# An attention round on TensorE: the transposes of the probabilities move behind the projections' step

## The chip, the core and the metric

The kernel runs on one core of one Trainium2 chip. The time is device microseconds of one execution of the whole kernel; lower is better. TensorE is called PE below, its weight loads PEld, VectorE DVE, ScalarE ACT, GpSimd POOL and SyncE SP, as in the profile.

## What is computed

One encoder layer with two parallel branches is applied to a prompt of 1024 tokens and, with the same weights, to a sample of 512 tokens; the model width is 1024. The part that the change touches is branch B, a windowed attention with three dilations (1, 4 and 16), 8 heads of width 64 each. Cut to what matters, for one dilation:

```python
logits = einsum('bghnqe,bghnke->bghnqk', qr, kb) + bias        # windows of 64 + 2*64 keys
mx = max(where(mask, logits, -inf), -1)
p = exp(logits - mx[..., None]); den = sum(p, -1)
o = einsum('bghnqk,bghnke->bghnqe', p, vb)                     # unnormalised; mixed over the dilations later
```

Around it stand one wide input projection `h @ w_in` (about 9700 columns), branch A (a bidirectional mLSTM scan in chunks of 128 tokens), gates, two output projections, a last projection and two RMS norms.

## The kernel before, in words

**Stages.** The prompt ("A", 1024 tokens) is projected first. From about 1000 us on, `body` (L1906 on) runs five stages in turn: mLSTM of A (L1951), attention of A (L1956), mLSTM of the sample "B" (L1967), attention of B (L1980), and the mixing of B's dilations with what is left (L1984 on). The two attention stages lie at about 1316 to 1636 us and 1846 to 2112 us of the span.

**Fill.** These stages have little work for PE between their dependent steps. So `Fill` (L114) holds a list of other units of work, projections of the sample and output projections of both inputs, each cut into steps; `fill(share)` (L171) advances a running target by a share of the stage's rate and issues as many steps as that makes due. One step is a product of three matmuls (`mm3`, L206: high by high, low by high and high by low part of fp32r pairs), of 512, 430 or 426 columns. A is given 260 steps for 96 rounds, B 290 for 48 (`STEPS`, L1751, and L1427). A unit of weights is loaded by DMA into `wraw` (L261), then split: ACT rounds it to `wh` (L272) and DVE subtracts (`wl`, L278). `split_w` (L264) makes the two wait in issue order for the last few attention instructions, which are kept in `held`.

**A tile of attention.** `attention` (L1304) makes tiles of 128 queries of two heads, with 256 keys ("wide": dilations 1 and 4 of A, dilation 1 of B) or 128 keys. Each has four stages:

- stage 0, `products` (L1354): on PE, the logits into the PSUM tile `lg` (L1362, or `mm3` through L209 to L211).
- stage 1, `softmax` (L1369): on DVE bias and maximum for each head (L1374) and the negated maximum `nm` (L1376); on ACT the two exponentials into `ls` (L1378).
- stage 2, `turn` (L1381): on PE 4 transposes (2 for a narrow tile) of `ls` into the PSUM tile `pt` (L1385); then one copy `pts` out of PSUM, on DVE for even tiles (L1390) and on ACT for odd ones (L1388).
- stage 3, `output` (L1393): on PE the products with the values into `o` (L1398), which read `pts`; on ACT the copy `ot` out of PSUM (L1400); then a DMA is queued.

**A round.** `attend` (L1408) appends one tile per round and calls `att_round` (L1473), which gives each of the last four tiles one stage: the newest its stage 0, the one before its stage 1, then 2 and 3; `fill(1)` is one more entry of that list. 12 units of 8 tiles make 96 rounds in A, 12 of 4 make 48 in B, and three more rounds drain the pipeline of each.

**What sets the order.** In these stages PE and SP keep the order in which the program issues (`manual_schedule`, L1907). DVE, ACT and POOL are put in order by a scheduler ahead of the run, by its own estimate of when each instruction can start; at run time every engine works through its list in order. `lg`, `pt` and `o` have two PSUM buffers each, `pts` two and `ls` three in SBUF. In attention A one more generator, `lanes` (L923), is advanced by four of the rounds (L1462): it works out the gates of B's mLSTM with small instructions on PE, ACT and DVE (L934 to L1008).

Of the kernel before, what the change touches and what calls it, by code (L numbers as in the profile page):

```python
# [181 lines left out]
class Net:  # L182
# [1289 lines left out]

    def att_round(self, tiles, fill):  # L1473

        for age, stage in ((0, 0), (1, 1), (2, 2), (None, None), (3, 3)):
            if age is None:
                fill(1)
            elif age < len(tiles) and tiles[-1 - age] is not None:
                tiles[-1 - age][stage]()
# [571 lines left out]
```

## Time and profile before

| what | value |
| --- | --- |
| time, three runs | 2256.5, 2256.57 and 2256.66 us (median 2256.57) |
| span of the profiled execution, first to last instruction | 2259.7 us, 3.1 us over the median of the timed runs |
| PE busy | 2244.2 us, 99% of the span |
| PEld, DVE, ACT, POOL busy | 1964.6, 1509.5, 1129.2, 718.6 us |
| granted PE clock | 1.000 |
| transposes L1385 in both attention stages | 71.9 us of PE (union of their records) |
| value products L1398 in both | 115.4 us of PE |
| PE idle in attention A, in attention B | 0.24 us of 320, 1.19 us of 266 |

The profile is of one execution. A row of its timeline has the start, the duration, the engine, the source line, the operation, the tile written and the tiles read, the shape, how many instructions were merged into the row, and in brackets how long the engine stood idle before it and what ended that. The duration of a matmul reaches to its modelled end, and the next one starts before it; what PE spends on one is read from start to start.

### The profile page before, as it was taken

The page shows a single profiled execution, that of the slowest core. Times are in us where ns is not written, and L with a number is a line of the kernel's source. Part 1 is how long each engine was busy: PE and PEld are TensorE (multiplying, and loading weights), DVE is VectorE, ACT ScalarE, POOL GpSimd, SP SyncE. Part 2 cuts the span into 40 slices and gives each one's busy share as a digit, 9 for nine tenths or more (in the row PEclk, how much of TensorE's full clock was granted, in tenths as well). Part 3 has the DMA queues.
Part 4 walks back from the last instruction along what each step waited for, and adds up shares of the span by engine and source line. Part 5 has one row for each costly group of instructions (what it writes and reads, how often), then busy time and mean ns, then how long its engine had stood idle before and what let it go on. Part 6 is the DMA issues. An engine that isn't in the chain of part 4 may idle for free.

```text
span 2259.7 us, 35388 instructions
## 1 busy us (share of the span) xinstructions
PE 2244.2 (99%) x12226; PEld 1964.6 (87%) x12226; DVE 1509.5 (67%) x2875; ACT 1129.2 (50%) x2369; POOL 718.6 (32%) x1000
## 2 busy tenths in 40 slices
PE   9999999999999999999999999999999999999998
PEld 8999888888888888888888899999888888888887
DVE  7765577687776556558887755544689844655674
ACT  6432244344444434357777655566665644554332
POOL 1000333333333223237676610011165522221221
PEclk9999999999999999999999999999999999999999
DMA  3652455543332223284664789997678797776663
GB/s 123 168 134 76 172 205 192 192 176 121 112 111 103 84 84 140 103 298 153 226 223 127 191 217 235 253 245 221 203 248 284 238 278 211 233 251 200 233 230 109
DMA packets 222685, 418.27 MB, mean 185 GB/s; under 512 B 24841, under 2 KB 128969, under 8 KB 222506
## 3 DMA queue, kind: packets, MB, share of 16 engines
q1 hardware_dynamic: 194536, 315.86, 44.4%
q0 software_dynamic: 24368, 87.56, 12.4%
q10 hardware_dynamic: 3602, 12.59, 1.4%
q8 instruction: 97, 1.59, 0.3%
q14 instruction: 82, 0.67, 0.1%
HBM read 296.19 MB, written 128.12 MB: 188 GB/s over the span
## 4 chain that ended last, share of the span: by engine, by line
PE 95%; DMA 2%; issue 1%; ACT 1%; POOL 1%; DVE 0%; DVEq 0%; SPq 0%; POOLq 0%; ACTq 0%
PE d L211 14%; PE d L209 14%; PE d L210 14%; PE dense L209 12%; PE dense L211 12%; PE dense L210 12%; PE o L1398 4%; PE pt L1385 2%; PE lg L1362 2%; PE num L211 1%; PE num L209 1%; PE num L210 1%; PE kv L209 1%; PE a L1070 1%; PE kv L210 1%
## 5 line engine op out<-in xcount | busy, mean ns | idle before, releaser
L209 PE MATMUL dense<-H,wh 128*128 128x512 f32 x664 | 270.6, 408 | 0.8 <-DVE V0b L1643 0.8
L211 PE MATMUL dense<-H,wl 128*128 128x512 f32 x664 | 260.9, 393 | 0.0
L210 PE MATMUL dense<-H,wh 128*128 128x512 f32 x664 | 260.2, 392 | 0.0
L210 PE MATMUL d<-Hl,phla 128*128 128x512 f32 x608 | 236.5, 389 | 0.0
L211 PE MATMUL d<-Hh,phla 128*128 128x512 f32 x608 | 236.5, 389 | 0.0
L209 PE MATMUL d<-Hh,phla 128*128 128x512 f32 x608 | 236.5, 389 | 0.0
L278 DVE TENSOR_TENSOR wl<-wraw,wh 128x1024 fp32r<-128x1024 f32 (+1 forms) x121 | 149.3, 1234 | 70.0 <-ACT wh L272 69.9
L1374 DVE CUSTOM_DVE_ANT_0 ls<-lg,bias 128x256 f32<-128x256 f32 (+1 forms) x288 | 93.7, 362 | 132.8 <-PE lg L1362 71.2
L211 PE MATMUL d<-Hh,phlb 128*128 128x512 f32 x456 | 177.4, 389 | 0.0
L209 PE MATMUL d<-Hh,phlb 128*128 128x512 f32 x456 | 177.4, 389 | 0.0
L210 PE MATMUL d<-Hl,phlb 128*128 128x512 f32 x456 | 177.4, 389 | 0.0
L687 POOL TENSOR_TENSOR psum_w<-pw_raw 128x512 f32<-128x512 f32 x38 | 58.0, 1527 | 365.1 <-DMA pw_raw<-w_in 208.8
L1378 ACT ACTIVATE ls<-ls,nm 128x256 f32<-128x256 f32 (+1 forms) x288 | 130.3, 454 | 84.0 <-DVE nm L1376 59.2
L272 ACT ACTIVATE wh<-wraw 128x1024 fp32r<-128x1024 f32 (+1 forms) x124 | 128.7, 1038 | 77.1 <-PE dense L210 27.0
L211 PEld LDWEIGHTS dense<-H,wl 128*128 128x128 f32 x664 | 124.6, 188 | 28.2
L209 PE MATMUL d<-vhi,Hh 128*128 128x322 f32 x448 | 140.9, 315 | 0.3
L211 PE MATMUL d<-vhi,Hl 128*128 128x322 f32 x448 | 140.3, 313 | 0.4 <-DVE Hl L396 0.2
L210 PE MATMUL d<-vlo,Hh 128*128 128x322 f32 x448 | 139.7, 312 | 0.0
L209 PEld LDWEIGHTS dense<-H,wh 128*128 128x128 f32 x664 | 125.0, 188 | 15.5 <-DVE V0b L1643 1.2
L210 PEld LDWEIGHTS dense<-H,wh 128*128 128x128 f32 x664 | 125.4, 189 | 14.3
L211 PEld LDWEIGHTS d<-Hh,phla 128*128 128x128 f32 x608 | 114.1, 188 | 23.7
L210 PEld LDWEIGHTS d<-Hl,phla 128*128 128x128 f32 x608 | 114.2, 188 | 23.6
(570 smaller groups left out, 6166.4 us busy)
## 6 DMA issues: line engine op xcount, KB each, us to landing
pw_raw<-w_in SPq DMA_DIRECT2D x76, 512.0 KB
wraw<-w_in SPq DMA_DIRECT2D x64, 512.0 KB
aqk_a<-pwk SPq DMA_DIRECT2D x48, 512.0 KB
aqk_b<-sw SPq DMA_DIRECT2D x48, 256.0 KB
wraw<-w_pm POOLq DMA_DIRECT2D x24, 512.0 KB, 6.1
wraw<-w_out POOLq DMA_DIRECT2D x24, 512.0 KB, 4.0
wraw<-w_v POOLq DMA_DIRECT2D x22, 430.0 KB, 7.3
erep<-erow SPq DMA_DIRECT2D x16, 512.0 KB
```

Of the source, the lines that this page charges most:

```text
L209: nc.tensor.matmul(out, lh, rh, start=start, stop=False)
L210: nc.tensor.matmul(out, lh, rl, start=False, stop=False)
L211: nc.tensor.matmul(out, ll, rh, start=False, stop=stop)
L272: high = nc.scalar.activation(hi[:, :n], raw[:, :n], AF.Copy)
L278: low = (self.lows or nc.vector).tensor_sub(lo[:, :n], raw[:, :n], hi[:, :n].bitcast(F32))
L687: self.nc.gpsimd.tensor_add(s[:, 0], ws[1][:, 0], ws[1][:, 1])
L1070: nc.tensor.matmul(p[:, c - c0], kT[:, ct, c * P:(c + 1) * P], qT[:, ct, c * P:(c + 1) * P], start=ct == 0, stop=ct == 1)
L1362: nc.tensor.matmul(lg[:, hh, c:c + w], q[hh][:, qs], z[:, k0:k0 + w], start=z is k[hh], stop=z is not k[hh])
L1374: nc.vector.tensor_tensor_reduce(out=ls[:, hh], in0=ts["lg"][hh], in1=bt[:, hh], scale=1.0, scalar=NEG, op0=OP.add, op1=OP.max, accum_out= ...
L1378: self.held = self.held[-3:] + [nc.scalar.activation(ls[:, hh], ls[:, hh], AF.Exp, bias=nm[:, hh:hh + 1], accum_out=ot[:, 128 + hh:129 + hh])]
L1385: nc.tensor.transpose(pp[:, hh * nk + x], ts["ls"][:, hh, x * P:(x + 1) * P], self.ident)
L1398: nc.tensor.matmul(po[:, hh * 64:hh * 64 + 64], pt[:, hh * nk + x], v[:, kt[x], c0 + hh * 64:c0 + hh * 64 + 64], start=x == 0, stop=x == n ...
```

## The change

One entry of the list in `att_round` moves. Before, PE's order in a round was logits of the newest tile, transposes of the tile two older, the projections' step (`fill(1)`), value products of the tile three older. After, it is logits, projections' step, transposes, value products. The stages' ages, the buffers, the DMAs and all shapes stay as they are.

```diff
     def att_round(self, tiles, fill):
 
-        for age, stage in ((0, 0), (1, 1), (2, 2), (None, None), (3, 3)):
+        for age, stage in ((0, 0), (1, 1), (None, None), (2, 2), (3, 3)):
             if age is None:
                 fill(1)
             elif age < len(tiles) and tiles[-1 - age] is not None:
                 tiles[-1 - age][stage]()
```

Compared instruction by instruction, the built programs have the same number of PE instructions with the transposes moved, SP's list is the same, and the lists of ACT, DVE and POOL hold the same work in a somewhat different order.

## The prediction

> **What bounds the kernel now.** I read the page's head, its chain of work, the busy time by stage, and PE's own waits.
>
> ```profile
> span 2259.7 us, 35388 instructions
> PE 95%; DMA 2%; issue 1%; ACT 1%; POOL 1%; DVE 0%; DVEq 0%; SPq 0%; POOLq 0%; ACTq 0%
> ```
>
> ```profile
> 1316.00:1636.00 320.00, 319.76 (x2157) 304.63 (x2156) 166.31 (x627) 204.39 (x637) 34.21 (x67) 1.00 0.88 234
> 1846.00:2112.00 266.00, 264.81 (x1426) 226.92 (x1427) 155.69 (x402) 132.55 (x362) 64.98 (x124) 1.00 0.72 223
> ```
>
> ```profile
> PE num L211 <- POOL scl L1110: 1.2, 1, 1.2
> PE dense L209 <- DVE V0b L1643: 0.8, 1, 0.8
> PE o L1398 <- ACT pts L1388: 0.2, 1, 0.2
> ```
>
> PE is 95% of the chain that ends last. The second fence has the two attention stages, its columns busy PE, PEld, DVE, ACT, POOL, then PE's clock and the DMA share: PE idles 0.24 us in A's stage and 1.19 us in B's. The third has what PE's waits say of these stages and the start of the mLSTM behind A's. So PE streams without a hole in nearly all of the 144 rounds (96 in A, 48 in B). A new order can gain only these 1.4 us, unless the matmuls themselves get cheaper side by side; it can lose wherever it opens a hole, one for one, since nothing but PE is on the chain. A reported time should follow the span: the profiled one is 2259.7 us, 3.1 us over the median of 2256.57 us, and I add the sum to the median.
>
> **What the change removes, adds and moves.** No instruction goes or comes. On PE the transposes pass the round's projection steps. Three costs follow: what PE pays at the new seams, what the value products wait for, and what the altered lists of ACT, DVE and POOL delay. SP's list, with every DMA that it issues, is unchanged.
>
> *Seams.* One round of A, PE's rows, the middle of the fill left out:
>
> ```profile
> 1400.12 1.00 PE L1398 MATMUL o<-K,pts 128*128 128x64 f32 x8
> 1400.93 0.36 PE L1362 MATMUL lg<-V1a,Q 128*128 128x256 f32 x1
> 1401.13 0.28 PE L1362 MATMUL lg<-V1b,Q 128*128 128x256 f32 x1
> ...
> 1401.48 0.60 PE L1385 MATMUL pt<-ident,ls 128*128 128x128 f32 x4
> 1401.84 0.44 PE L209 MATMUL dense<-wh,H 128*128 128x430 f32 x1
> 1402.12 0.36 PE L210 MATMUL dense<-wl,H 128*128 128x430 f32 x1
> 1402.32 0.36 PE L211 MATMUL dense<-wh,H 128*128 128x430 f32 x1
> ```
>
> Steady, a 430-column matmul takes 0.20 us from start to start (1402.12 to 1402.32). From the first transpose to the second step matmul lie 0.64 us (1401.48 to 1402.12); less 0.20 for the first step matmul, 0.44 is left: 0.11 for each of four transposes, the last too. From the first value product to the second logits matmul lie 1.01 us; less 0.12 for the first logits matmul (256 columns), 0.89 is left, 0.11 for each of eight. So the group pays its own slots and no more on leaving. The seam that the change makes, transposes straight into f32 products, is found in the opening stage:
>
> ```profile
> 35.58 0.27 PE L428 MATMUL d<-ident,x 128*128 128x128 f32 x1
> 35.69 0.39 PE L430 MATMUL d<-Hl,x 128*128 128x128 f32 x2
> 35.91 0.27 PE L428 MATMUL d<-ident,x 128*128 128x128 f32 x1
> 36.02 0.39 PE L430 MATMUL d<-Hl,x 128*128 128x128 f32 x2
> ```
>
> There a transpose (L428) and an f32 product (L430, two records) take turns, 0.33 us for the three, 0.11 each: no price in either direction. The seams are taken at 0; the bounds are in the rivals.
>
> *What the products wait for.* They need `pts`, copied out of PSUM after the transposes. Before, two fills lie between transposes and products of a tile; after, one.
>
> ```profile
> 1404.47 0.60 PE L1385 MATMUL pt<-ident,ls 128*128 128x128 f32 x4
> 1406.67 1.00 PE L1398 MATMUL o<-K,pts 128*128 128x64 f32 x8
> 1410.23 0.33 PE L1398 MATMUL o<-K,pts 128*128 128x64 f32 x2
> ```
>
> ```profile
> 1405.36 0.69 DVE L1390 COPY pts<-pt 128x512 f32<-128x512 f32 x1
> ```
>
> This tile's transposes start at 1404.47, its copy ends at 1406.05 (1.58 us later, and that behind DVE's softmax of another tile), its products start at 1410.23. After, the transposes stand just ahead of the other tile's products, 0.44 us before 1406.67, at 1406.23: 4.00 us are left for 1.58, so 2.4 us are spare. The narrow rounds of A are shortest:
>
> ```profile
> 1551.71 0.55 PE L1398 MATMUL o<-K,pts 128*128 128x64 f32 x4
> 1552.51 0.38 PE L1385 MATMUL pt<-ident,ls 128*128 128x128 f32 x2
> 1553.89 0.56 PE L1398 MATMUL o<-K,pts 128*128 128x64 f32 x4
> ```
>
> ```profile
> 1553.23 0.42 DVE L1390 COPY pts<-pt 128x256 f32<-128x256 f32 x1
> ```
>
> From transposes to end of copy 1.14 us; a round of 2.18 us plus 0.22 for the two transposes gives 2.40, spare 1.26. B's rounds last 5.5 us on the mean (266 by 48), so more is spare. In an ordinary round the change costs nothing, and what hides the copy is one fill in place of two. In exchange the exponentials get a fill more ahead of the transposes, which no PE wait asks for.
>
> *Where one fill doesn't do.* A late copy already shows once, where the `lanes` work sits on ACT:
>
> ```profile
> 1465.59 0.58 ACT L1388 ACTIVATE pts<-pt 128x512 f32<-128x512 f32 x1
> 1466.56 0.51 ACT L1378 ACTIVATE ls<-ls,nm 128x256 f32<-128x256 f32 x1 [0.39 <-DVE nm L1376]
> ...
> 1467.56 0.26 ACT L1400 ACTIVATE ot<-o 128x128 f32<-128x128 f32 x1
> ...
> 1473.21 1.28 ACT L945 ACT_TABLE_LOAD   x1
> 1474.51 0.31 ACT L945 ACTIVATE l_e<-l_l 64x128 f32<-64x128 f32 x1
> 1474.72 0.58 ACT L1388 ACTIVATE pts<-pt 128x512 f32<-128x512 f32 x1
> 1475.25 0.51 ACT L1378 ACTIVATE ls<-ls,nm 128x256 f32<-128x256 f32 x1
> ...
> 1476.25 0.26 ACT L1400 ACTIVATE ot<-o 128x128 f32<-128x128 f32 x1
> ```
>
> ```profile
> 1475.35 1.10 PE L1398 MATMUL o<-K,pts 128*128 128x64 f32 x8 [0.24 <-ACT pts L1388]
> ```
>
> The products at 1475.35 start as this copy ends (1474.72 and 0.58). In the changed program's list the copy stands behind the two exponentials of the tile two younger, which take 1475.25 to 1476.25: 1.0 us later. The copy of two tiles earlier (1465.59) likewise moves behind its two exponentials, out of a place with 0.39 us of idle time behind it ahead of work that may run without a gap to 1474.72: by an estimate from those rows about 0.5 us more for all behind it. Together PE waits about **1.5 us** longer here. Between 0.9 (the second shift absorbed) and 2.4 us (the tile of the first copy misses its products too, by one more evicting instruction). Behind the late products on PE stand the next logits and steps; who waits for those is late by as much, and PE's stream is simply shifted.
>
> *POOL's list.* It differs in three places; one is near PE, where B's mLSTM begins.
>
> ```profile
> 1639.58 0.59 POOL L250 DMA_DIRECT2D sraw<-ym_a  x1 [9.30 <-ACT st L1072]
> ...
> 1641.94 0.46 POOL L1110 TENSOR_TENSOR scl<-rm,sch 128x128 fp32r<-128x128 f32 x1 [0.57 <-ACT sch L1109]
> ...
> 1643.40 1.44 POOL L1118 TENSOR_TENSOR ql<-qw,qh 128x256 fp32r<-128x256 f32 x2 [0.63 <-ACT qh L1117]
> ```
>
> ```profile
> 1644.26 0.28 PE L211 MATMUL num<-V0a,scl 128*128 128x258 f32 x1
> ```
>
> After, the DMA issue that waits until 1639.58 stands ahead of the first mask and product, and one `ql` ahead of that `scl`. `ql` can't start before about 1643.3 (here it waits for ACT until 1643.40), takes 0.72, then `scl` 0.46: 1644.5 or later, against a need at 1644.26. I take **0.4 us**, between 0 and 1.0.
>
> *Sum.* 1.5 + 0.4 = 1.9 us on 2259.7, or 2258.5 on the median: 0.08% more. A measurement here can tell about 0.2%, 4.5 us, from no change.
>
> **The rivals.**
>
> *Copies queue behind late weights (slower).* Place: the copies on ACT, which in the new list follow exponentials and, in several rounds, a weight split (L272) that waits for its DMA. In A's stage ACT's waits have this row:
>
> ```profile
> ACT wh L272 <- DMA wraw<-w_v: 8.8, 3, 3.3
> ```
>
> Two fills cover such a wait; of the 2.4 us that are spare with one, a wait of 3.3 and the two exponentials behind it (1.0) leave about 2 us open. It decides when a copy ends more than a round after its transposes begin. Three such places and the 1.9 make 2256.6 + 1.9 + 6 = 2264.5 us. Against it: in the list the copies of two of the three places stand behind by less than what is spare.
>
> *The seam costs (slower).* If a transpose streamed like the logits, 0.12 us for 256 columns, it would need 0.06 for its 128; a load of 0.11 behind it would then show in the new seam, 0.05 us in each of 144 rounds: 7 us, 2265.5 with the 1.9. Against it stand the 0.44 us for four transposes in front of step matmuls and the alternating rows. The Trainium skill says so in "TensorE: Matmul & The Clock Gate": by "LDWEIGHTS (loading the stationary operand)" and "Weight-path perf modes — Fast Weight Load (FWL) and DoubleRow", f32 weights get no fast load and 128 columns take an estimated 107 ns, by "Back-to-back issue gap" 128 columns stream in about 56. The trace disagrees for f32 transposes: 110 ns, whatever is loaded next.
>
> *The seam gains (faster).* The first step matmul after the transposes shows 0.44 and 0.28 us to the next, the first logits matmul 0.36 and 0.20: some 0.08 us over the usual. If that were paid for each change from f32 to fp32r, the change would save one of two per round, 144 times 0.08 = 11.5 us: 2247. Against it: the matmul is recorded early by as much, and the sums above leave nothing.
>
> *Nothing happens.* ACT's list turns out to hide the copy at 1475, POOL is in time: 2256.6.
>
> **How the numbers follow.** Forecast 0.56 (its own range 2257.0 to 2260.5), nothing 0.15, late weights 0.16, seam costs 0.06, seam gains 0.07. Faster by over 0.2% (under 2252.1): the seam gain, 0.07. Slower by over 0.2% (over 2261.1): the two slower ones, 0.22. Within: 0.71. The range for 8 in 10 holds forecast and nothing (0.71), and reaches up into the late weights: 2256.0 to 2264.5.
>
> **What would show it.** Right: in the order of time, value products start 0.44 us after the first of four transposes; PE's busy time and the two L1398 and L1385 groups are unchanged; PE's wait for `pts` grows from 0.2 to about 1.7 us, all near 1475, and the wait of `num` for `scl` stands near 1644. Wrong: waits of `o` for `pts` in many rounds, or a distance other than 0.11 us per transpose at the new seam.

## The result and the profile after

| kernel | runs | median (lowest to highest) | ratio to before, 95% interval |
| --- | --- | --- | --- |
| before, beside the first runs of after | 15 | 2256.66 us (2256.35 to 2260.06) | |
| after | 15 | 2261.24 us (2260.16 to 2264.55) | 1.0017 [1.0010, 1.0024] |
| after, second time (e4) | 11 | 2262.07 us (2258.46 to 2268.26) | 1.0019 [1.0010, 1.0028] |
| after, third time (e11) | 11 | 2261.66 us (2259.60 to 2270.83) | 1.0015 [1.0006, 1.0024] |

The change makes the kernel slower by 0.15 to 0.19%. Over all 108 runs of before and 37 of after that stood beside each other the medians are 2258.53 and 2261.66 us, 3.1 us apart. One kernel's own runs spread over 6 us and more, so no single profile may be subtracted from another: the first profile of after has a span of 2260.9 us, only 1.2 us more than the one of before.

Of the profile after, first the head of the page and the chain, then the two attention stages (columns as before: busy PE, PEld, DVE, ACT, POOL, then clock and DMA share), then PE's waits:

```profile
span 2260.9 us, 35348 instructions
...
PE 92%; DMA 3%; issue 2%; POOL 1%; ACT 1%; DVE 1%; SPq 0%; DVEq 0%; POOLq 0%; ACTq 0%
```

```profile
1316.00:1636.00 320.00, 319.57 (x2154) 299.83 (x2153) 171.99 (x628) 202.21 (x637) 33.11 (x65) 1.00 0.87 233
...
1846.00:2112.00 266.00, 263.93 (x1425) 223.94 (x1425) 158.03 (x402) 133.74 (x362) 64.79 (x124) 1.00 0.75 226
```

```profile
PE dense L209 <- ACT sw L896: 1.7, 1, 1.7
PE num L211 <- POOL scl L1110: 1.4, 2, 1.2
...
PE o L1398 <- ACT pts L1388: 0.4, 1, 0.4
PE dense L209 <- ACT K L1662: 0.4, 1, 0.4
```

PE still streams: 0.43 us of idle time in A's attention (0.24 before), 2.07 in B's (1.19 before). Most of the 2.07 is the wait for `sw` at 1847, 1.7 us here and 0.7 in the profile of before; the other two profiles of after don't have it, so this one can't be laid to the change. What is new is a handful of single waits. The products wait for `pts` in one round out of 144, no longer at 1475 but at 1344; one of the two waits for `scl` is new; so is the one for `K` (L1662). The wait for `V0b` at 2026 is gone.

The seams, PE's rows of one round of after:

```profile
1399.25 0.60 PE L1385 MATMUL pt<-ident,ls 128*128 128x128 f32 x4
1399.69 1.00 PE L1398 MATMUL o<-K,pts 128*128 128x64 f32 x8
...
1401.25 0.36 PE L210 MATMUL dense<-wl,H 128*128 128x430 f32 x1
```

Four transposes take 0.44 us, as forecast (1399.25 to 1399.69). The three groups, up to the second step matmul, take 2.00 us (1399.25 to 1401.25); in the round of before that the prediction shows they took 2.00 us too (1400.12 to 1402.12). Counted from the start of the last step matmul ahead of the three groups, which adds its slot of 0.196 us, the medians over the 53 rounds of this shape are 2.195 us before and 2.192 after. The new order costs PE nothing at its seams.

**The wait at 1344.** ACT's rows of after, then DVE's, then PE's:

```profile
1340.20 0.92 ACT L272 ACTIVATE X<-wraw 128x860 fp32r<-128x860 f32 x1 [2.42 <-DMA wraw<-w_v]
1342.38 0.51 ACT L1378 ACTIVATE ls<-ls,nm 128x256 f32<-128x256 f32 x1 [1.26 <-DVE nm L1376]
...
1343.39 0.57 ACT L1388 ACTIVATE pts<-pt 128x512 f32<-128x512 f32 x1
```

```profile
1341.15 1.05 DVE L278 TENSOR_TENSOR X<-wraw,X 128x860 fp32r<-128x860 f32 x1 [1.87 <-ACT X L272]
1342.13 0.16 DVE L1376 TENSOR_SCALAR nm<-ot 128x2 f32<-128x2 f32 x1
```

```profile
1342.98 0.60 PE L1385 MATMUL pt<-ident,ls 128*128 128x128 f32 x4
1344.01 1.10 PE L1398 MATMUL o<-K,pts 128*128 128x64 f32 x8 [0.43 <-ACT pts L1388]
```

Read it backwards. PE's products wait for the copy `pts`. ACT makes it only at 1343.39, because two exponentials stand ahead of it in its list; they wait for `nm`; on DVE `nm` stands behind the subtraction of a weight split; and that stands behind ACT's half of the split, which waited 2.42 us for its DMA. The copy's own input was ready by the end of the transposes at about 1340.5 (they are on PE from 1340.01). In before, ACT made this copy ahead of the split and of the exponentials, and on DVE `nm` stood ahead of the subtraction (1341.58); ACT's rows, then DVE's:

```profile
1340.13 0.60 ACT L1388 ACTIVATE pts<-pt 128x512 f32<-128x512 f32 x1 [1.14 <-PE pt L1385]
1340.63 0.91 ACT L272 ACTIVATE X<-wraw 128x860 fp32r<-128x860 f32 x1
1341.44 0.50 ACT L1378 ACTIVATE ls<-ls,nm 128x256 f32<-128x256 f32 x1
```

```profile
1340.54 0.27 DVE L1376 TENSOR_SCALAR nm<-ot 128x2 f32<-128x2 f32 x1
```

The split starts no later in after (1340.20) than in before (1340.63). So the weights did not come later; what changed is what stands behind them.

**The wait near 1644.** POOL's rows of after, then PE's:

```profile
1638.87 0.55 POOL L250 DMA_DIRECT2D sraw<-ym_a  x1 [13.15 <-ACT st L1072]
...
1642.76 0.74 POOL L1118 TENSOR_TENSOR ql<-qw,qh 128x256 fp32r<-128x256 f32 x1 [1.13 <-issue]
1643.45 0.46 POOL L1110 TENSOR_TENSOR scl<-rm,sch 128x128 fp32r<-128x128 f32 x1
```

```profile
1643.97 0.39 PE L211 MATMUL num<-V0a,scl 128*128 128x258 f32 x1 [0.24 <-POOL scl L1110]
```

The DMA issue now comes ahead of the first mask, one `ql` ahead of `scl`, and PE starts 0.41 us late: the matmul before it started at 1643.44 and its slot is 0.12 us. (The 0.24 in brackets counts from the modelled end of that matmul, so it is less than what start to start shows. That holds for all such brackets on PE.)

### The profile page after: what moved, and what is told of

The parts are those of the page before. It is cut to its first block, busy times and chain, and to the rows that moved or that the text cites. A ratio compares the mean times of both kernels' runs of the same rounds, so it can differ in the third digit from the quotient of the medians.

```text
span 2260.9 us, 35348 instructions
## 1 busy us (share of the span) xinstructions
PE 2244.3 (99%) x12226; PEld 1958.1 (87%) x12226; DVE 1516.9 (67%) x2875; ACT 1126.5 (50%) x2369; POOL 715.2 (32%) x1000
## 4 chain that ended last, share of the span: by engine, by line
PE 92%; DMA 3%; issue 2%; POOL 1%; ACT 1%; DVE 1%; SPq 0%; DVEq 0%; POOLq 0%; ACTq 0%
PE d L211 14%; PE d L209 14%; PE d L210 14%; PE dense L209 11%; PE dense L211 11%; PE dense L210 11%; PE o L1398 4%; PE pt L1385 2%; PE lg L1362 2%; PE num L211 1%; PE num L209 1%; PE num L210 1%; PE kv L209 1%; PE kv L210 1%; PE kv L211 1%
```

## The experiments

"Trace from the logits on" is the time from the first logits of A's attention (first L1362) to PE's last matmul. It leaves out the 1315 us ahead of it, where no order changes and where executions of these kernels differ by 4 us (1314.2 to 1318.4 us).

### Again, and one stage alone

e1 is the kernel before, e4 the one after, unchanged. e2 and e3 take the new order in one stage only:

```
-        for age, stage in ((0, 0), (1, 1), (2, 2), (None, None), (3, 3)):
+        moved = T.n > 4          # e2: A's attention; e3: T.n <= 4, B's
+        for age, stage in (((0, 0), (1, 1), (None, None), (2, 2), (3, 3)) if moved else
+                           ((0, 0), (1, 1), (2, 2), (None, None), (3, 3))):
```

> The kernel before, unchanged, as one more kernel beside itself. Ratio 1.000. Its profile is a second execution of the same program: it shows which of the single holes in PE's stream of the first profile (0.24 us at 1475 for pts, 0.8 us at 2026 for V0b, 0.9 us at 1846 for sw) come in every execution and which in one only. Theory 'single holes' (the 4.6 us between the medians are a handful of waits for copies and weights): this profile has fewer of them than the first, because its span should be near 2255 us and not 2259.7. Theory 'paid in every round' (the new seam): its holes are the same and PE's busy time is lower by 4 us than in the profile after.

> The new order in the prompt's attention alone (96 of 144 rounds), the old one in the sample's. Theory 'paid in every round': two thirds of the 4.6 us, some 3 us, with no hole in PE's stream. Theory 'single holes': what it loses stands as holes by 1343 us (0.4 us, pts behind exponentials that wait for late value weights), 1644 us (0.4 us, scl) and no more, so 0 to 1.5 us in all, and the hole at 1475 us is gone.

> The new order in the sample's attention alone (48 rounds), the old one in the prompt's. Theory 'paid in every round': a third, some 1.5 us. Theory 'single holes': the holes at 1847 us (1.7 us in the profile after, for sw) and 1965 us (0.4 us, for K) belong here, so 1 to 3 us; the hole for pts at 1475 us is as before.

> The changed kernel once more, on the chip of the three others. 1.0015 to 1.002 of the time before. Its profile shows which holes of the first profile after (1343, 1644, 1739, 1847, 1965 us) come again. Theory 'single holes': the sum of holes over the 1000 to 2112 us, less the same sum of the kernel before in this call, equals the difference of the times within 1 us. Theory 'paid in every round': the sums are equal and the start-to-start time at the new seam is longer.

| | ratio | trace from the logits on | new waits |
| --- | --- | --- | --- |
| e1 | 0.9996 [0.9987, 1.0005] | 936.1 us | none |
| e2, A alone | 1.0012 [1.0003, 1.0021] | 936.1 us | `pts` 0.9 us in two places, `scl` 0.40 near 1647 |
| e3, B alone | 1.0002 [0.9994, 1.0011] | 935.3 us | `K` 0.6 us |
| e4 | 1.0019 [1.0010, 1.0028] | 936.6 us | `pts` 0.7, `scl`, `K` 0.5 us |

The waits come again where the new order is and only there: `pts` at 1344 and `scl` at 1644 with A's, `K` with B's. By the medians nearly all of the loss belongs to A (2262.04 us in e2, 2262.07 in e4, 2259.38 in e3, beside 2258.71 of before), by the ratios about two thirds; e2's one profile doesn't show a loss from the logits on (936.1 us, as in e1). The expectation that the sum of holes equals the difference of the times can't be tested on one pair: e1's profiled execution took 2260.71 us, the second longest of its eleven, e4's 2260.57, the second shortest. e1 also had a 0.8 us wait for a DMA that the other profiles of before don't have. "Paid in every round" fails: PE's rows and its busy time show nothing of it.

### How much cover the copy needs

e6 puts the transposes behind the products of the older tile, e7 gives a tile's transposes and its products to the same round:

```
 after: ((0, 0), (1, 1), (None, None), (2, 2), (3, 3))
 e6:    ((0, 0), (1, 1), (None, None), (3, 3), (2, 2))
 e7:    ((0, 0), (1, 1), (None, None), (2, 2), (2, 3))
```

> Transposes one place later still, behind the value products of the older tile: logits, projections' step, value products, transposes. Between a tile's transposes and its products there are then the next logits and one fill: 1.34 us less than in the changed kernel in a wide round, 0.66 less in a narrow one. By the rows of before 1.1 us are still spare in a wide round and 0.6 in a narrow one, so an ordinary round should still wait for nothing: theory 'single holes' gives 2 to 10 us over the changed kernel, all of it as waits of o for pts. Theory 'the cover is already used up' gives a wait in most rounds, 30 us or more.

> No fill at all between a tile's transposes and its products: they follow each other in the same round. This prices the cover itself. A wide round should wait from the end of its transposes to the end of the copy, 1.58 less 0.44, 1.14 us, a narrow one 1.14 less 0.22, 0.92 us: 80 wide rounds and 64 narrow ones make 150 us. More, if the copies stand behind other work of DVE and ACT in many rounds; under 100 us if they are reached sooner than in the rows that were read.

e6: 1.0012 [1.0003, 1.0021], 2260.36 us; e7: 1.0779 [1.0764, 1.0793], 2434.6 us. PE's waits, first of e6, then of e7:

```profile
PE o L1398 <- ACT pts L1388: 3.2, 4, 1.1
...
PE o L1398 <- DVE pts L1390: 1.7, 1, 1.7
```

```profile
PE o L1398 <- ACT pts L1388: 66.4, 72, 2.7
PE o L1398 <- DVE pts L1390: 58.0, 71, 1.6
```

With no fill between, 143 of 144 rounds wait, 0.87 us each on the mean by the brackets. From start to start, less the last transpose's slot of 0.109 us, it is 1.03 us in each of the 144 rounds, 149 us in all, so the expectation (0.92 to 1.14 us, 150 in all) was right for the wait. The time grew by 176 us; about 15 more were lost in 31 us at half the clock, the rest is not told apart. e6 has one fill and the next logits as cover, 1.34 us less than after in a wide round, and five rounds of 144 wait. So an ordinary round has room to spare with one fill, as the rows of before said. e6 waits more than after but isn't slower; its PE was busy 5.6 us less than before, which the expectation had not foreseen.

### The order on PE, or the lists of the other engines

e5 keeps the new order on PE, and puts the copies back ahead of the next softmax. e9 keeps the old order on PE, and puts the copies behind the exponentials of the tile two younger, as in after:

```
 e5:  softmax: nm and the exponentials under
+        with self.tc.issue_after(self.copied.ins) if self.copied else ExitStack():
      turn:
+        self.copied = last
 e9:  turn keeps the transposes and hands its copy on; softmax of the next round calls it at its end, under
+        with self.tc.issue_after(self.exps.ins):
```

> The changed order on PE, but the scheduler is told to put each copy pts ahead of the next softmax's nm and exponentials, as it stood in the lists of before. Theory 'lists' (the change costs because the copies now stand behind two exponentials, which wait for nm and late weights): the holes of o for pts near 1344 and 1475 us are gone, POOL's list still has the late scl at 1644 (0.4 us), so about 1 us less than the changed kernel: 2 to 3 us over the kernel before. Theory 'distance' (one fill is too short for the copy wherever its place in the list): the holes stay, the time is that of the changed kernel.

> The order on PE of before (two fills between transposes and products), but each copy pts issued behind the exponentials of the tile two younger, so that the lists of ACT, DVE and POOL are nearly those of the changed kernel. Theory 'one fill and late lists together': no wait of o for pts, because the second fill covers the late copy; the scl hole of 0.4 us at 1644 us is there, since POOL's list has it; 0 to 2 us over the kernel before. Theory 'the lists alone': the time of the changed kernel, 3 to 4 us over before. Theory 'PE's order alone': the kernel before.

| | copies ahead of the exponentials | copies behind them |
| --- | --- | --- |
| two fills (old order on PE) | before, 1 | e9, 1.0020 [1.0011, 1.0028] |
| one fill (new order on PE) | e5, 1.0006 [0.9997, 1.0015] | after, 1.0015 to 1.0019 |

The column decides, not the row: e9 loses as much as after with PE's order untouched. (e5 and after did not run beside each other, and e5's interval reaches up to after's lowest ratio; it is their profiles that separate them.) e9's lists of ACT and POOL are nearly those of after, DVE's is closer to that of before, and its profile has the same waits: for `pts` at 1345 (0.57 us) and 1478, for `scl` at 1651. In e5's profile the list of PE's waits has none for `pts`; its `scl` wait is there, because POOL's list has not gone back. At 1344 ACT waits for the same weights and splits them at 1341.60, later than in after, yet the copy comes right behind, at 1342.42, and PE doesn't wait. The place near 1475, ACT's rows of e5 and the products that need the copy:

```profile
1473.92 0.58 ACT L1389 ACTIVATE pts<-pt 128x512 f32<-128x512 f32 x1
```

```profile
1475.02 1.00 PE L1400 MATMUL o<-K,pts 128*128 128x64 f32 x8
```

The same place in e9, ACT's rows, PE's, and three stretches of time (the last three columns are PE's clock, the DMA share and GB/s):

```profile
1476.85 0.51 ACT L1378 ACTIVATE ls<-ls,nm 128x256 f32<-128x256 f32 x1 [0.43 <-DVE nm L1376]
...
1477.85 0.57 ACT L1395 ACTIVATE pts<-pt 128x512 f32<-128x512 f32 x1
```

```profile
1478.47 1.87 PE L1411 MATMUL o<-K,pts 128*128 128x64 f32 x8 [1.98 <-ACT pts L1395]
```

```profile
1478.40:1480.40 2.00, 1.93 (x9) 1.93 (x10) 1.97 (x10) 0.18 (x2) 0.00 (x0) 0.55 1.09 383
1480.40:1484.40 4.00, 4.00 (x15) 3.84 (x15) 1.01 (x6) 2.88 (x11) 0.00 (x0) 0.50 0.70 195
1484.40:1486.40 2.00, 2.00 (x13) 1.92 (x13) 0.00 (x0) 0.53 (x2) 0.00 (x0) 0.74 0.31 110
```

Here the wait is 1.98 us, and then PE runs at about half its clock for some seven: 0.45 of 2.0, 0.50 of 4.0 and 0.26 of 2.0 us are lost, 3.4 us more. The trace of e9 from the logits on is 940.7 us. Its eleven times lie in two groups, 2259.7 to 2261.6 and 2263.6 to 2266.2 us. Such a clock dip is not what parts them: the profiled execution (2265.79 us) has a mean clock of 0.998, but two others of the slower group (2265.48 and 2265.61) have 1.000, and two of the faster one 0.998. What does stays open.

### Transposes first, and the price of leaving the products

e8 takes the transposes to the head of the round. e10 has the same four groups with the fill behind the products:

```
 e8:  ((2, 2), (0, 0), (1, 1), (None, None), (3, 3))
 e10: ((0, 0), (1, 1), (2, 2), (3, 3), (None, None))
```

> Transposes first in the round: transposes, logits, projections' step, value products. The copy has the logits and two fills, more than in the kernel before, and the exponentials have 0.5 us less than before ahead of the transposes. Theory 'the copy's cover decides': within 1 us of the kernel before, no hole of o for pts. Theory 'exponentials are the tight side': waits of pt for ls, several us slower.

> A test of what the run with the transposes first showed: its PE was busy 7 us less, because the value products there are followed by transposes and not by logits. Order here: logits, transposes, value products, projections' step; the products are followed by a step matmul. Theory 'leaving the value products into any long matmul costs some 55 ns': PE is busy 2244 us as before, and the interval from the last product to the second step matmul is 55 ns over its two slots. Theory 'only the way into the logits costs': PE is busy 2237 us and the kernel is 3 to 5 us faster, less what the waits for pts take (one fill and the logits lie between transposes and products).

e8 is faster than both kernels: 2253.72 us, 0.9981 [0.9972, 0.9990], 927.9 us from the logits on, where the three profiles of before have 935.5 on the mean. It has no wait for `pts` and none near 1644, as expected, but that would make it equal to before at best. The rest is PE's work itself. The page's line of busy time, then a round:

```profile
PE 2237.4 (99%) x12226; PEld 1959.0 (87%) x12226; DVE 1514.7 (67%) x2875; ACT 1124.8 (50%) x2369; POOL 714.7 (32%) x1000
```

```profile
1399.60 1.00 PE L1398 MATMUL o<-K,pts 128*128 128x64 f32 x8
1400.44 0.61 PE L1385 MATMUL pt<-ident,ls 128*128 128x128 f32 x4
1400.80 0.36 PE L1362 MATMUL lg<-V1a,Q 128*128 128x256 f32 x1
1401.00 0.28 PE L1362 MATMUL lg<-V1b,Q 128*128 128x256 f32 x1
...
1401.55 0.36 PE L210 MATMUL dense<-wl,H 128*128 128x430 f32 x1
```

The three groups take 1.95 us (1399.60 to 1401.55) in place of 2.00. In cyclic order this is products, transposes, logits, fill, which is e6's order too. Median start-to-start times of the 53 rounds of this shape say where the 0.05 lies. From the first product to the second it is 55 ns in place of 112, when a long matmul stood ahead (58 behind a transpose, in after). From the last product into logits it is 84 to the first logits matmul and 202 to the next, against 117 for an ordinary one: 57 ns over the two slots. So the group gains 57 on entering and pays 57 on leaving; the prediction saw only the sum, and called it no price. From the last product into a transpose it is 112, and 115 to the next, against 109 for an ordinary one: 6 ns. From the last transpose into logits, 28 and 202, 4 ns over its two slots: next to nothing in both. A round of e8 saves some 50 ns, which in 144 of them would be 7.2 us; PE is busy 6.8 us less than in the profile of before. The gain by the times is smaller, 4.3 us with an interval from 2.3 to 6.3.

e10 asks whether it is the logits that cost. PE's rows:

```profile
1402.10 1.00 PE L1398 MATMUL o<-K,pts 128*128 128x64 f32 x8
1402.91 0.44 PE L209 MATMUL dense<-wh,H 128*128 128x430 f32 x1
1403.20 0.36 PE L210 MATMUL dense<-wl,H 128*128 128x430 f32 x1
```

Products into a step matmul: by the medians 84 and 280 ns, 56 over the two slots (112 and 196). So leaving the products costs into a step matmul as into the logits, and its PE is busy 2247.2 us. Its time is 1.0017 [1.0008, 1.0026]. The profiled execution was the longest of its ten (2268.23 us); it has a wait of 3.3 us for `sw` (L1706) with half a clock behind it, and two waits for `pts`, 1.5 us near 1476 and 0.5 near 2036.

### A third time

> The changed kernel a third time, for its size beside that of the kernel before on one chip: 1.001 to 1.0025. Its profile should again have a wait of o for pts near 1344 us (0.4 to 0.8 us) and the scl hole of 0.4 us at 1644 us; from the first logits to the end it should take 936.6 to 938.6 us as in its other two profiles.

> The kernel before a third time: ratio 1.000; from the first logits to the end 936 us as in its other two profiles, with no wait at 1344 and none at 1644 us.

e11: 1.0015 [1.0006, 1.0024], 936.8 us from the logits on; e12: 0.9997 [0.9988, 1.0006], 934.3 us. e12 has no wait at 1344, 1475 or 1644; e11 has all three, the one at 1475 now of the forecast size. ACT's and PE's rows of e11, and the same two places on ACT in the first profile of after, which did not wait:

```profile
1467.56 0.34 ACT L936 ACTIVATE l_li<-o,gb 32x128 f32<-32x128 f32 x1
...
1474.41 0.49 ACT L1378 ACTIVATE ls<-ls,nm 128x256 f32<-128x256 f32 x1
...
1475.39 0.57 ACT L1388 ACTIVATE pts<-pt 128x512 f32<-128x512 f32 x1
```

```profile
1476.02 0.32 PE L1398 MATMUL o<-K,pts 128*128 128x64 f32 x1 [1.35 <-ACT pts L1388]
```

```profile
1465.74 0.34 ACT L936 ACTIVATE l_li<-o,gb 32x128 f32<-32x128 f32 x1
...
1473.58 0.58 ACT L1388 ACTIVATE pts<-pt 128x512 f32<-128x512 f32 x1
```

From the first `lanes` instruction to the copy it is 7.83 us in e11 and 7.84 in after: ACT has no gap there. Only the start differs, 1467.56 or 1465.74, and PE wants the copy at about 1474.5. What sets the start is a weight split that waits for its DMA, first in e11, then in after:

```profile
1462.94 0.92 ACT L272 ACTIVATE wh<-wraw 128x860 fp32r<-128x860 f32 x1 [3.06 <-DMA wraw<-w_v]
```

```profile
1461.12 0.92 ACT L272 ACTIVATE wh<-wraw 128x860 fp32r<-128x860 f32 x1 [1.26 <-DMA wraw<-w_v]
```

From the start of this split to the copy it is 12.45 and 12.46 us, and 12.44 in e4 (1461.71 to 1474.15): ACT works through one chain behind the weights, and the wait on PE grows as they come later (1.23 us later in e11 than in e4, and the wait 1.28 us longer over the slots). So it is in the kernel before: the first profile, with a wait of 0.24 us for `pts` there, has the latest split (1463.62, behind a wait of 3.29 us); e1 and e12 have it at 1461.66 and 1461.99 and no such wait. In e5 the chain is 1.2 us shorter (1462.70 to 1473.92). The old place of the copy was ahead of the two exponentials, 1.0 us earlier.

## Why the prediction was right, and where it was not

The median of 2261.24 us lies in the range (2256.0 to 2264.5), and the loss of 0.15 to 0.19% on the side that was forecast; the forecast case's own range (2257.0 to 2260.5) was passed by 0.7 us, and 1.9 us were forecast where 3.1 to 4.6 came. That the range held the time is in part luck: it does so because it was stretched towards a rival, and the sum itself was short.

- **Seams at 0: right.** 2.00 us for the three groups in both orders. The reason given was half true: the products do pay for leaving, and gain as much on entering. Both seams stay in this change; e8 shows what it is worth to lose one. The rows that it read for the new seam have products of 128 moving columns, 0.11 us each; the first product of 64 behind a transpose takes 58 ns in place of 112. The rival "the seam gains" looked for its saving where transposes meet step matmuls, where nothing is paid.
- **Ordinary rounds wait for nothing: right.** One or two rounds of 144 wait in the three profiles of after; e6, with still less cover, has five.
- **`lanes`, 1.5 us: the place and the order of the list right, the size not one number.** Nothing, 0.23 and 1.51 us over the slots in three executions, two of them under the bound of 0.9. The prediction took the start of ACT's run from one profile; it moves by 1.8 us between executions, with the landing of the weights that ACT waits for just ahead.
- **POOL's `scl`, 0.4 us: right.** 0.40 to 0.41 us in each profile of after, of e2 and of e5, and in none of before.
- **Late weights: taken as a rival at three places of 2 us, it is part of the result.** One place, 1344, in every profile of after: 0.43, 0.65 and 0.83 us by the brackets. This is the term that the sum lacked. The three waits for `w_v` in the row that the prediction quotes belong to other weights (`wh`); the longest of them, 3.29 us, is the one ahead of `lanes`, so rival and forecast shared a cause. The wait of 2.42 us at 1344 is a fourth, for `X`. Before shows no such wait because ACT was busy with the copy until 1340.63; the weights are no later now. What hurts is that the copy stands behind the split and the exponentials, and these behind DVE's `nm`, which stands behind the split too.
- **"What hides the copy is one fill in place of two": wrong as the cause.** e9 has two fills and loses the same; e5 has one and loses 0.06%, with an interval that reaches zero. The list that the scheduler made, with the copy behind work that waits, is the cause; the distance on PE alone costs nothing that can be measured. Nor do two fills cover such a wait, as the rival assumed: with two, e9's products wait 0.57 and 1.98 us.
- **Not foreseen:** `K` (L1662) near 1965, 0.4 to 0.8 us, while `V0b` near 2026, 0.5 to 0.8 us in each profile of before, is gone (by e2 and e3 the first comes with B's new order, the second goes with A's; how was not followed); and the clock, which can make a wait of 2 us cost more than 5.

What stays open: from the logits on, the three profiles of after are on the mean 1.8 us longer than the three of before (937.3 and 935.5 us), which is about the sum that was forecast, but made up of other waits. The medians differ by 3.1 us. Three profiles a side can't place the missing 1.3, since those of one kernel differ by 2 us among themselves (934.3 to 936.2 and 936.6 to 938.6). Clock dips could explain the longest times of after, 2268.26 and 2270.83 us, whose mean clock is 0.998, but only one more execution of the 37 has that clock, and three don't move a median.

## What to carry to other kernels

When a line moves in a program that a scheduler orders, first compare the lists of the engines that were not meant to change: what a move costs can lie in an instruction that slipped behind another one's wait, its size then moves with that wait from one execution to the next, and it can be tried by itself, with the order on the main engine kept. Then price each seam of the main engine from both ends, what a group pays on entering and on leaving: a zero sum hides a price, and one that can be avoided by what is put next to it (here 50 ns in 144 rounds, and a kernel 0.2% faster than before).

## What the runs showed of the hardware

A gap in PE's stream of about 2 us can halve its clock for some microseconds afterwards. In e9 it was 1.98 us, and the clock was halved for 6.8. In e2, in a stage that the change does not touch, PE's row and a stretch behind it:

```profile
999.98 0.39 PE L211 MATMUL num<-V0a,scl 128*128 128x258 f32 x1 [2.04 <-POOL scl L1110]
```

```profile
1002.00:1004.00 2.00, 2.00 (x9) 1.90 (x8) 0.48 (x1) 1.82 (x5) 0.00 (x0) 0.50 1.01 386
```

The gap of 3.31 us in e10 did it too. Gaps of 1.35 us (e11) and 1.73 us (after, `sw`, up to 1847.59) left the clock at 1.00. The length of the gap alone doesn't decide, as e7 shows: gaps of 1.53 us (up to 1454.16) and 1.58 us (up to 2168.19) were followed by half a clock, and one of 2.74 us was not. Its row, and a stretch behind it:

```profile
1532.27 1.10 PE L1398 MATMUL o<-K,pts 128*128 128x64 f32 x8 [2.74 <-ACT pts L1388]
```

```profile
1532.30:1538.00 5.70, 4.92 (x36) 4.57 (x37) 1.66 (x7) 1.65 (x6) 0.00 (x0) 1.00 0.06 15
```

The dips of e7 start at 1350.05, 1455.86, 1551.43, 1571.91, 1978.10 and 2169.24 us, whole multiples of 3.413 us apart, and each lasts one, two or three such steps. The gaps of 1.53, 1.98 (e9) and 2.04 us (e2) lie within the one step that ends where the dip starts; the gap of 2.74 us lies across the end of a step, with 1.42 and 1.32 us in the two. So the idle time in one step seems to decide, but no clear limit comes out: steps with up to 1.73 us kept the clock, and one with 1.44 us in several gaps (e7, ahead of 1350.05) lost it.

The Trainium skill, "TensorE: Matmul & The Clock Gate", section "Part 1: The HAM clock gate (the "warmup" mystery)", tells of a half-rate state that follows an idle window of about 3.4 us. The half rate agrees, and so does the step of 3.413 us; but here gaps of about 2 us inside one were enough, so by these runs that figure is no safe limit for a gap.
